# A compression of overlapping blocks in a two-layer attention trunk: each token stored once, and three weight chunks split earlier

## The chip, the cores and the metric

The kernel runs on one core of one Trainium2 chip. The metric is the time of one execution in microseconds (us), the median of several runs. Before the change it is 596.03 us (three runs, 595.75 to 596.15).

The core has five engines that work side by side, each through its own queue in order: TensorE (PE) multiplies matrices, with a separate unit for loading the stationary operand (PEld); VectorE (DVE), ScalarE (ACT) and GpSimd (POOL) work element by element; SyncE (SP) issues most of the DMA transfers.

## The reference

A trunk of two layers on 256 tokens of width 1024, in float32. Layer 0 is sparse latent attention with a squared-ReLU MLP. After it a shared key/value side is computed once from the normalized stream `hs`; layer 1 (attention over compressed, selected and window keys, again with an MLP) reads it. The change lies in that shared side:

```
kv = (hs @ w_kv).reshape(B, T, 6, N_KV_GROUPS, HEAD_DIM)
k_cmp, v_cmp, k_slc, v_slc, k_win, v_win = [kv[:, :, i] for i in range(6)]
kc = compress_blocks(k_cmp, n_cmp, pos_k, w1_k, w2_k)
vc = compress_blocks(v_cmp, n_cmp, pos_v, w1_v, w2_v)
...
def compress_blocks(raw, n_cmp, pos, w1, w2):
    idx = CMP_STRIDE * np.arange(n_cmp)[:, None] + np.arange(CMP_LEN)[None, :]
    blocks = raw[:, idx] + pos[None, None, :, None, :]
    flat = ...                       # (B, n_cmp, groups, CMP_LEN * HEAD_DIM)
    return jax.nn.gelu(flat @ w1) @ w2
```

There are 15 blocks of 32 tokens, each starting 16 tokens after the one before, so a token lies in two blocks (at place l and at place l - 16). Two groups make 30 blocks for the keys and 30 for the values. `w1` has 32 x 128 rows and 256 columns.

## The kernel before

Every float32 product is made of three matmuls: each operand is split into a rounded part (`h`, a cast on ScalarE) and a remainder (`l`, a subtraction on VectorE, `x - h`), and `h*h + h*l + l*h` is summed in PSUM (`mm3`). A weight chunk of 128 x 1024 is loaded by SyncE into one of five raw buffers (`rawp`), cast by ScalarE, and its remainder is taken by VectorE into one of eight buffers (`wp`). A raw buffer is free for the next load when the remainder has been written. The program order is made by a scheduler on the basis of its own costs; `behind(a, b)` lays down that `a` stands behind `b` on its engine.

The shared side runs as follows (function `trunk`):

- `kk`: keys of the selected and window branches, 96 matmuls with the four chunks `wk`; the scale `Rb` per token comes from the sum of squares of `x2`.
- The `xns` loop (line 850): eight products of `x2` by `Rb` on GpSimd into two alternating buffers, each split into `ah` (ScalarE) and `al` (VectorE), which the gates and the queries of layer 1 read later.
- `Ks` (lines 857 to 863): `kf` = `kk` times `Rb` on VectorE, cast on ScalarE, remainder on GpSimd.
- For kv = 0 (keys) and 1 (values), line 869: `kc`, 48 matmuls with the chunks `wc` into a bank of 512 columns (two groups of 256 tokens). `ff` (line 879) copies them out, times `Rb`, sorted by place in the block: for each of 32 places 30 columns of blocks, one of the position vector (line 881) and one of zeros. Four products of 16 x 15 elements do that, since each token stands at two places. `fr` holds the cast and the remainder of `ff`, 64 columns to a place; `fl` is a copy of the last place with 64 zero columns behind it, because a matmul takes 128 columns.
- `compress(kv, c, co)` (line 892): eight chunks of `cmp_w1`, of four places each. A place is one matmul: 128 columns of `fr` stationary, 512 columns (cast and remainder of the weights) moving, all summed in the bank `co`. Of the 128 result rows the first 64 are wanted. In the trace `c` are the split weights, `c1raw` their raw buffers. The remainders of kv 0's chunks 1 to 7 stand behind the remainder of `fr` of kv 0 (`frl[0]`).
- Behind it the V projection: four chunks `wv` of 12 matmuls each in the banks `v`, and between them kv 1's eight compression chunks. `compressed` copies 64 rows of `co` out (`cs`), and `hidden` sums the rows that belong together with the 0/1 matrix `sel` (matmuls `hp`), then the gelu; `kcT` is the compressed key.
- Then the gates (`gps`, 16 matmuls), the queries (`nq`, chunks `wq`) and the attention of layer 1.

`turn_gates` also uses `sel`, to sum two rows of each gate.

Of the kernel before, what the change touches and what calls it, by code (L numbers as in the profile page):

```python
# [50 lines left out]
def trunk(ctx: ExitStack, tc: tile.TileContext, I, out):  # L51
    nc = tc.nc
    const = ctx.enter_context(tc.tile_pool(name="const", bufs=1))
# [140 lines left out]
    def bcast(col2, name):  # L194

        ps = bank(name + "_ps")
        for i in range(2):
            mm(ps[:, i * P:(i + 1) * P], col2[:, i:i + 1].to_broadcast([P, P]), ident,
               i == 0, i == 1)
        b = kept([P, T], name)  # L200
        nc.vector.tensor_copy(b, ps[:, :T])
        return b
# [47 lines left out]
    for j in range(4):  # L250
# [8 lines left out]
        else:  # L259
# [4 lines left out]
            for a in range(2):  # L264
                g = vec[:, V_GA + 2 * j + a:V_GA + 2 * j + a + 1]
# [3 lines left out]
        for i in range(2):  # L269
            for a in range(2):  # L270
                k = 2 * j + a
# [23 lines left out]
    for j in range(2):  # L295
# [3 lines left out]
    pos = const.tile([P, 2, 32], F32, name="pos")  # L299
    pin(nc.sync.dma_start(pos, I["pos"]))  # L300
    pin(nc.sync.dma_start(biasT, bass.AP(tensor=u_ap.tensor, offset=u_ap.offset,
                                         ap=[[1, P], [384, H], [1, T]])))
    sel = const.tile([64, 32], F32, name="sel")
    pin(nc.sync.dma_start(sel, I["sel"]))


# [99 lines left out]
    for a in range(2):  # L406
        g = vec[:, V_GQ + a:V_GQ + a + 1]
# [361 lines left out]
    x1 = bigt([P, KT, T], F32, "x1")  # L769
# [9 lines left out]
    for fi in range(NF):  # L779
# [8 lines left out]
        if fi == 14:  # L788


            ps = bank("m1_ps")
# [9 lines left out]
        if 18 <= fi < 26:  # L801
            k = fi - 18
# [30 lines left out]
    for k in range(KT):  # L833
# [12 lines left out]
        if k == 6:  # L846
            Rb = bcast(r2, "Rb")

    xns = wk("cs", 1, [P, 2, T], "xns")
    for k in range(KT):  # L850
        xn = xns[:, k % 2]
        nc.gpsimd.tensor_tensor(xn, x2[:, k], Rb, op=OP.mult)
        hi, lo = split_gain(ah, al, x2, V_GA + 8, k, xn)
        behind(hi, kw_last[0])
        behind(lo, kw_last[1])
    Ks = bigt([P, 2, G, 2, T], F32R, "Ks")

    kf = x1[:, 4:].rearrange("p (g a) t -> p g a t", g=G)
    for g in range(G):
        nc.vector.tensor_tensor(kf[:, g], kk[g].rearrange("p (a t) -> p a t", a=2),  # L860
                                Rb[:, None, :].to_broadcast([P, 2, T]), op=OP.mult)
    nc.scalar.copy(Ks[:, 0], kf)
    nc.gpsimd.tensor_sub(Ks[:, 1], kf, f(Ks[:, 0]))


    w2 = wk("w2", 1, [P, 2, 2, P], "w2")
# [1 line left out]
    frs, frl = [], []  # L868
    for kv in range(2):
        ps = bank(f"kc{kv}")  # L870
        for g in range(G):
            projT(ps[:, g * T:(g + 1) * T], cw[2 * kv + g], sh, sl, g == 0)

        ff = x1[:, 4 * kv:4 * kv + 4].rearrange("p k t -> p (k t)").rearrange("p (l c) -> p l c", c=32)
        pv = ps.rearrange("p (g c b) -> p b g c", g=G, b=16)
        rv = Rb.rearrange("p (c b) -> p b c", b=16)
        for a in range(2):
            for g in range(G):
                nc.vector.tensor_tensor(ff[:, 16 * a:16 * a + 16, NCMP * g:NCMP * (g + 1)],
                                        pv[:, :, g, a:a + NCMP], rv[:, :, a:a + NCMP], op=OP.mult)  # L880
        nc.vector.tensor_copy(ff[:, :, 30:31], pos[:, kv, :, None])
        nc.vector.memset(ff[:, :, 31:32], 0.0)

        fr = bigt([P, 32, 2, 32], F32R, f"fr{kv}")
        nc.scalar.copy(fr[:, :, 0], ff)
        frl.append(nc.vector.tensor_sub(fr[:, :, 1], ff, f(fr[:, :, 0])))
        fl = wk("fl", 2, [P, 4, 32], f"fl{kv}", F32R)
        nc.gpsimd.memset(fl[:, 2:].bitcast(mybir.dt.int32), 0)
        nc.vector.tensor_copy(fl[:, :2], f(fr[:, 31]))
        frs.append((fr.rearrange("p l s c -> p (l s c)"), fl.rearrange("p s c -> p (s c)")))  # L890

    def compress(kv, c, co):
        fr, fl = frs[kv]
        raw = rawp.tile([P, 1024], F32, tag="raw", name=f"c1raw{kv}{c}")
        nc.sync.dma_start(raw, I["cmp_w1"][kv, c])
        w = wp.tile([P, 2, 1024], F32R, tag="w", name=f"c1{kv}{c}")
        w4 = w.rearrange("p a (b c) -> p (a b) c", c=512).rearrange("p l (s n) -> p l s n", s=2)
        r4 = raw.rearrange("p (l n) -> p l n", n=256)
        nc.scalar.copy(w4[:, :, 0], r4)
        lo = nc.vector.tensor_sub(w4[:, :, 1], r4, f(w4[:, :, 0]))  # L900
        if kv == 0 and c > 0:
            behind(lo, frl[0])
        for j in range(4):
            l = 4 * c + j
            mm(co, fr[:, 64 * l:64 * l + P] if l < 31 else fl, w4[:, j].rearrange("p s n -> p (s n)"),
               l == 0, l == 31)

    def compressed(kv, co):
        cs = wk("cs", 1, [64, 512], f"cs{kv}")
        nc.scalar.copy(cs, co[:64])  # L910
        return cs

    def hidden(kv, cs):
# [17 lines left out]
    co = [bank(f"co{kv}", acc=True) for kv in range(2)]  # L931
    for c in range(8):
        compress(0, c, co[0])
# [7 lines left out]
    for c in range(4):  # L941
        h, l = weights(I["kvV"][c], f"wv{c}")
        for i in range(2):
            for j in range(2):
                k = 2 * c + j
# [10 lines left out]
    ps = bank("kcT_ps")  # L956
# [11 lines left out]
    w4 = w[:, 0, :KT * 64].rearrange("p (k s c) -> p k s c", s=2, c=32)  # L968
# [7 lines left out]
    gT = wk("grep", 1, [64, T], "gT")  # L976
# [3 lines left out]
    def turn_gates():  # L980

        gtp = bank("gtp")
        for i in range(2):
            mm(gtp[:, i * 32:i * 32 + 24], gT[:, i * P:(i + 1) * P], sel[:, :24], i == 0, i == 1)
        gflat = gate.rearrange("p i h c -> p i (h c)")
        for i in range(2):
            nc.scalar.activation(gflat[:, i], gtp[:, i * 32:i * 32 + 24], AF.Exp, scale=-1.0)
        nc.vector.tensor_scalar(gflat, gflat, 1.0, None, op0=OP.add)
        nc.vector.reciprocal(gflat, gflat)
# [167 lines left out]
    ps = bank("vc_ps")  # L1157
# [4 lines left out]
    pv = ps[:, :T].rearrange("p (g d) -> p g d", g=G)  # L1162
# [45 lines left out]
    for fi in range(NF):  # L1208
# [14 lines left out]
        if 16 <= fi < 20:  # L1223
            i, c = divmod(fi - 16, 2)
            ps = bank(f"x3t{i}{c}")
# [19 lines left out]
    for i in range(2):  # L1245
        for c in range(2):
# [5 lines left out]
            if c == 0:  # L1252
                ins = nc.gpsimd.tensor_tensor(xg[:, i], x4[:, i, :512], gf[:, 0, :512], op=OP.mult)
# [27 lines left out]
def _const_arrays():  # L1281
    c = np.zeros((P, NC_), np.float32)
    c[:, C_ID:C_ID + P] = np.eye(P)
    p = np.arange(P)[:, None]
    s = np.arange(T)[None, :]
    c[:, C_CM:C_CM + T] = np.where(s > P + p, NEG, 0.0)
    n = np.arange(NCMP)[None, :]
    for i in range(2):
        ok = 16 * n + 31 <= i * P + p
        c[:, C_CA + 15 * i:C_CA + 15 * (i + 1)] = np.where(ok, 0.0, NEG)  # L1290
        c[:, C_C1 + 15 * i:C_C1 + 15 * (i + 1)] = ok
    for a in range(2):
        c[:, C_OWN + a] = 0.5 * (np.arange(P) % 32 // 16 == a)

    dist = np.arange(256)
    bucket = np.where(dist < 16, dist, 0)
    for b, lo in enumerate((16, 23, 32, 46, 64, 91, 128, 182)):
        bucket = np.where(dist >= lo, 16 + b, bucket)
    oh = np.zeros((32, 256), np.float32)
    oh[bucket, dist] = 1.0  # L1300
    sel = np.zeros((64, 32), np.float32)
    for j in range(30):
        sel[j, j] = sel[32 + j, j] = 1.0
    sel[30, :30] = sel[62, :30] = 1.0
    return c, oh, sel


# [72 lines left out]
```

## Time and profile before

| | |
|---|---|
| median of three runs | 596.03 us (595.75 to 596.15) |
| profiled execution | 595.66 us, of which 593.9 us are the span of the trace |
| TensorE busy | 577.7 us (97%) |
| VectorE, ScalarE, GpSimd busy | 366.2, 320.7, 155.9 us |
| granted TensorE clock | 0.998 of full speed |
| DMA | 103.96 MB, mean 175 GB/s |

A busy share says how long an engine had an instruction in it; a matmul whose operand comes late can count as busy. "Idle before" an instruction names what ended the wait. The chain that ended last follows the work back from the last instruction, at each step to what released it.

### The profile page before, as it was taken

The numbers are of one execution on the slowest core, as the hardware profiler recorded it, in microseconds if no ns is written. First come the engines' busy times: TensorE is split into PE (matmuls) and PEld (weight loads), VectorE is DVE, ScalarE is ACT, GpSimd is POOL, SyncE is SP. The second block draws the span as 40 slices with busy tenths as digits, with TensorE's granted clock in tenths as the row PEclk, the third lists the DMA queues.
The fourth block names the chain that finished last, engine by engine and source line by source line (L and its number), as shares of the span: only waits on it lengthen the run. The fifth ranks groups of instructions, "written<-read, shape, count | busy, mean of one in ns | idle before, by whom it ended". The sixth has DMA issues, their size and how long they took to land.

```text
span 593.9 us, 10855 instructions
## 1 busy us (share of the span) xinstructions
PE 577.7 (97%) x4170; PEld 542.6 (91%) x4170; DVE 366.2 (62%) x621; ACT 320.7 (54%) x580; POOL 155.9 (26%) x226
## 2 busy tenths in 40 slices
PE   8999999999999999999979999999999999999995
PEld 6788899999999999999958999999899998999994
DVE  4897399444475454447897877739845444444523
ACT  6656666454444444446576778627544445454423
POOL 0155466011011101014510067808410101011012
PEclk9999999999999999999999999999999999999999
DMA  8911448766556655544289843213866665566201
GB/s 306 338 51 57 162 159 256 240 179 187 174 160 197 201 175 187 178 142 159 73 302 315 318 174 108 78 66 129 278 205 185 195 183 173 181 178 197 84 1 71
DMA packets 30483, 103.96 MB, mean 175 GB/s; under 512 B 3640, under 2 KB 5472, under 8 KB 30304
## 3 DMA queue, kind: packets, MB, share of 16 engines
q1 hardware_dynamic: 30032, 102.45, 53.2%
q10 hardware_dynamic: 400, 0.83, 0.5%
q8 instruction: 32, 0.52, 0.3%
q14 instruction: 19, 0.16, 0.1%
HBM read 102.21 MB, written 1.06 MB: 174 GB/s over the span
## 4 chain that ended last, share of the span: by engine, by line
PE 84%; DVE 9%; issue 2%; DMA 2%; ACT 2%; POOL 1%; SPq 1%; POOLq 0%; ACTq 0%; DVEq 0%
PE y L94 30%; PE u L94 28%; PE nq L94 4%; PE yb L94 3%; PE ya L94 3%; PE kk L94 2%; PE npo L94 2%; PE v L94 1%; PE nl L94 1%; PE co L94 1%; DMA win_raw<-in_a_w_in 1%; PE kc L94 1%; PE ix L94 1%; DVE c L900 1%; DVE h0l L160 1%
## 5 line engine op out<-in xcount | busy, mean ns | idle before, releaser
L142 DVE TENSOR_TENSOR dn<-dn_raw,dn 128x1024 fp32r<-128x1024 f32 x64 | 80.7, 1260 | 99.1 <-ACT dn L141 99.1
L645 POOL TENSOR_TENSOR us<-ur 128x256 f32<-128x256 f32 x64 | 45.2, 708 | 282.2 <-ACT ur L642 282.2
L142 DVE TENSOR_TENSOR up<-up_raw,up 128x1024 fp32r<-128x1024 f32 x64 | 82.5, 1289 | 45.1 <-ACT up L141 45.1
L141 ACT CAST up<-up_raw 128x1024 fp32r<-128x1024 f32 x64 | 67.0, 1047 | 60.6 <-PE y L94 58.3
L94 PE MATMUL u<-h1h,up 128*128 128x256 f32 x512 | 97.0, 284 | 0.6 <-DVE up L142 0.6
L94 PE MATMUL y<-uu,dn 128*128 128x256 f32 x768 | 97.0, 283 | 0.2 <-DVE uu L647 0.2
L94 PE MATMUL u<-h0h,up 128*128 128x256 f32 x512 | 96.7, 283 | 0.0
L94 PEld LDWEIGHTS y<-uu,dn 128*128 128x128 f32 x768 | 94.2, 192 | 0.5 <-DVE uu L647 0.5
L94 PE MATMUL y<-dn,uu 128*128 128x512 f32 (+1 forms) x396 | 92.5, 384 | 0.0
L94 PEld LDWEIGHTS u<-h1h,up 128*128 128x128 f32 x512 | 81.5, 191 | 1.6 <-DVE up L142 0.8
L94 PEld LDWEIGHTS y<-dn,uu 128*128 128x128 f32 x396 | 71.1, 189 | 13.0
L642 ACT ACTIVATE ur<-u 128x256 f32<-128x256 f32 x64 | 24.5, 383 | 106.8 <-PE u L94 106.8
L94 PEld LDWEIGHTS u<-h0h,up 128*128 128x128 f32 x512 | 81.7, 192 | 0.0
L94 PE MATMUL u<-h1l,up 128*128 128x256 f32 x256 | 72.5, 283 | 0.0
L94 PE MATMUL u<-h0l,up 128*128 128x256 f32 x256 | 72.2, 283 | 0.0
L141 ACT CAST dn<-dn_raw 128x1024 fp32r<-128x1024 f32 x64 | 66.8, 1043 | 7.3 <-PE y L94 2.9
L94 PEld LDWEIGHTS u<-h1l,up 128*128 128x128 f32 x256 | 49.0, 191 | 0.9
L94 PEld LDWEIGHTS u<-h0l,up 128*128 128x128 f32 x256 | 49.1, 192 | 0.0
L647 DVE TENSOR_TENSOR uu<-us,uu 128x256 fp32r<-128x256 f32 x64 | 29.1, 454 | 8.1 <-POOL us L645 8.1
L646 ACT ACTIVATE uu<-ur 128x256 fp32r<-128x256 f32 x64 | 26.7, 417 | 0.1
L94 PE MATMUL ya<-oT,wo 128*128 128x256 f32 x192 | 25.2, 288 | 0.3 <-DVE oT L591 0.3
L94 PE MATMUL yb<-nTh,wn 128*128 128x256 f32 x128 | 24.7, 284 | 0.1
(304 smaller groups left out, 966.8 us busy)
## 6 DMA issues: line engine op xcount, KB each, us to landing
up_raw<-in_w_up SPq DMA_DIRECT2D x64, 512.0 KB, 3.7
dn_raw<-in_w_down SPq DMA_DIRECT2D x64, 512.0 KB, 3.7
c1raw<-in_cmp_w SPq DMA_DIRECT2D x16, 512.0 KB, 4.7
wo_raw<-in_a_w_o SPq DMA_DIRECT2D x8, 512.0 KB, 4.3
wq_raw<-in_b_w_q SPq DMA_DIRECT2D x8, 512.0 KB, 6.0
wn_raw<-in_b_w_o SPq DMA_DIRECT2D x8, 512.0 KB, 4.9
wk_raw<-in_kvT SPq DMA_DIRECT2D x4, 512.0 KB, 3.6
wc_raw<-in_kvT SPq DMA_DIRECT2D x4, 512.0 KB, 3.6
```

What stands on the lines that cost most here:

```text
L94: return nc.tensor.matmul(ps, a, b, start=start, stop=stop, skip_group_check=True)
L141: ins = [hi(w[:, 0, :C], raw[:, :C]) if hi else nc.scalar.copy(w[:, 0, :C], raw[:, :C]), (lo or nc.vector).tensor_sub(w[:, 1, :C], raw[:, ...
L142: (lo or nc.vector).tensor_sub(w[:, 1, :C], raw[:, :C], f(w[:, 0, :C]))]
L160: nc.vector.scalar_tensor_tensor(dst_l[:, k], x, g, f(dst_h[:, k]), op0=OP.mult, op1=OP.subtract))
L642: nc.scalar.activation(r, ps[:, :T], AF.Relu)
L645: nc.gpsimd.tensor_tensor(s, r, r, op=OP.mult)
L646: nc.scalar.activation(u[:, 0], r, AF.Square)
L647: nc.vector.tensor_sub(u[:, 1], s, f(u[:, 0]))
L900: lo = nc.vector.tensor_sub(w4[:, :, 1], r4, f(w4[:, :, 0]))
```

## The change

The tokens are sorted by their place modulo 16 and stored once: `ff` is one product of 16 x 2 x 16 elements, with two position columns (places l and l + 16) behind each 32, thus 34 columns for each of 16 places. `fr` has 17 rows of 2 x 34 columns, the last of zeros. Place l of the blocks reads 128 columns from `68 * (l % 16) + l // 16`: for l from 16 on the window is shifted by one column, which is the next block. The wanted rows become 68, and `sel` is rebuilt for them (with columns of its own for the gates). `fl` goes. The remainder of `Ks` is taken on VectorE. The remainders of kv 0's chunks 1 and 2 need no longer stand behind `frl[0]`; `al` from the third on stands behind it, and from the fifth on behind `frl[1]`; kv 1's `ff` stands behind `frl[0]`.

```diff
-    sel = const.tile([64, 32], F32, name="sel")
+    sel = const.tile([68, 56], F32, name="sel")
...
+    als = []
     for k in range(KT):
         xn = xns[:, k % 2]
         nc.gpsimd.tensor_tensor(xn, x2[:, k], Rb, op=OP.mult)
         hi, lo = split_gain(ah, al, x2, V_GA + 8, k, xn)
         behind(hi, kw_last[0])
         behind(lo, kw_last[1])
+        als.append(lo)
...
     nc.scalar.copy(Ks[:, 0], kf)
-    nc.gpsimd.tensor_sub(Ks[:, 1], kf, f(Ks[:, 0]))
+    nc.vector.tensor_sub(Ks[:, 1], kf, f(Ks[:, 0]))
...
-        ff = x1[:, 4 * kv:4 * kv + 4].rearrange("p k t -> p (k t)").rearrange("p (l c) -> p l c", c=32)
-        pv = ps.rearrange("p (g c b) -> p b g c", g=G, b=16)
-        rv = Rb.rearrange("p (c b) -> p b c", b=16)
-        for a in range(2):
-            for g in range(G):
-                nc.vector.tensor_tensor(ff[:, 16 * a:16 * a + 16, NCMP * g:NCMP * (g + 1)],
-                                        pv[:, :, g, a:a + NCMP], rv[:, :, a:a + NCMP], op=OP.mult)
-        nc.vector.tensor_copy(ff[:, :, 30:31], pos[:, kv, :, None])
-        nc.vector.memset(ff[:, :, 31:32], 0.0)
-
-        fr = bigt([P, 32, 2, 32], F32R, f"fr{kv}")
-        nc.scalar.copy(fr[:, :, 0], ff)
-        frl.append(nc.vector.tensor_sub(fr[:, :, 1], ff, f(fr[:, :, 0])))
-        fl = wk("fl", 2, [P, 4, 32], f"fl{kv}", F32R)
-        nc.gpsimd.memset(fl[:, 2:].bitcast(mybir.dt.int32), 0)
-        nc.vector.tensor_copy(fl[:, :2], f(fr[:, 31]))
+        ff = x1f[:, 544 * kv:544 * (kv + 1)].rearrange("p (b c) -> p b c", c=34)
+        ins = nc.vector.tensor_tensor(ff[:, :, :32].rearrange("p b (g c) -> p b g c", g=G),
+                                      ps.rearrange("p (g c b) -> p b g c", g=G, b=16),
+                                      Rb.rearrange("p (c b) -> p b c", b=16)[:, :, None, :].to_broadcast([P, 16, G, 16]),
+                                      op=OP.mult)
+        if kv:
+            behind(ins, frl[0])
+        nc.vector.tensor_copy(ff[:, :, 32:34], pos[:, kv].rearrange("p (a b) -> p b a", a=2))
+
+        fr = bigt([P, 17, 2, 34], F32R, f"fr{kv}")
+        nc.gpsimd.memset(fr[:, 16].bitcast(mybir.dt.int32), 0)
+        nc.scalar.copy(fr[:, :16, 0], ff)
+        frl.append(nc.vector.tensor_sub(fr[:, :16, 1], ff, f(fr[:, :16, 0])))
+        for lo in als[2 + 2 * kv:]:
+            behind(lo, frl[kv])
...
-        if kv == 0 and c > 0:
+        if kv == 0 and c > 2:
             behind(lo, frl[0])
         for j in range(4):
             l = 4 * c + j
-            mm(co, fr[:, 64 * l:64 * l + P] if l < 31 else fl, w4[:, j].rearrange("p s n -> p (s n)"),
+            o = 68 * (l % 16) + l // 16
+            mm(co, fr[:, o:o + P], w4[:, j].rearrange("p s n -> p (s n)"),
                l == 0, l == 31)
```

VectorE's queue before, from chunk 0's remainder to chunk 3's (`c_3494` is chunk 0 of kv 0, `c_3503` chunk 1, `c_3512` chunk 2, `c_3521` chunk 3; `x_850` holds `kf` and `ff`):

```order
L900 TENSOR_TENSOR c_3494<-c1raw_3492,c_3494 128x4x256
L201 COPY Rb<-Rb_ps 128x256
L860 TENSOR_TENSOR x_850<-kk_3186,Rb 128x512
L860 TENSOR_TENSOR x_850<-kk_3187,Rb 128x512
L160 SCALAR_TENSOR_TENSOR al<-xns,vec,ah 128x256 x2
L879 TENSOR_TENSOR x_850<-kc_3368,Rb 128x16x15 x4
L160 SCALAR_TENSOR_TENSOR al<-xns,vec,ah 128x256 x2
L886 TENSOR_TENSOR fr_3423<-x_850,fr_3423 128x32x32
L881 COPY x_850<-pos 128x32
L900 TENSOR_TENSOR c_3503<-c1raw_3501,c_3503 128x4x256
L900 TENSOR_TENSOR c_3512<-c1raw_3510,c_3512 128x4x256
L900 TENSOR_TENSOR c_3521<-c1raw_3519,c_3521 128x4x256
```

The same piece of VectorE's queue now (chunks 0 to 3 are `c_3482`, `c_3491`, `c_3500`, `c_3509`):

```order
L903 TENSOR_TENSOR c_3482<-c1raw_3480,c_3482 128x4x256
L201 COPY Rb<-Rb_ps 128x256
L903 TENSOR_TENSOR c_3491<-c1raw_3489,c_3491 128x4x256
L863 TENSOR_TENSOR x_850<-kk_3186,Rb 128x512
L863 TENSOR_TENSOR x_850<-kk_3187,Rb 128x512
L903 TENSOR_TENSOR c_3500<-c1raw_3498,c_3500 128x4x256
L160 SCALAR_TENSOR_TENSOR al<-xns,vec,ah 128x256 x2
L866 TENSOR_TENSOR Ks<-x_850,Ks 128x1024
L879 TENSOR_TENSOR x_850<-kc_3368,Rb 128x16x32
L885 COPY x_850<-pos 128x16x2
L890 TENSOR_TENSOR fr_3419<-x_850,fr_3419 128x16x34
L160 SCALAR_TENSOR_TENSOR al<-xns,vec,ah 128x256 x2
```

The remainders of chunks 1 and 2 moved from behind `fr` to between `Rb` and the first `al`, the `Ks` remainder came onto this queue, and four `ff` products became one.

TensorE's queue where the first `wv` chunk is used, before (`v_3567` and `v_3568` are the two V banks; `fr` of kv 0 is stationary in `co_3490`):

```order
L94 MATMUL co_3490<-c_3539,fr_3423 128x512 x4
L94 MATMUL v_3567<-wv_3571,sh 128x512
L94 MATMUL v_3568<-wv_3571,sh 128x512
L94 MATMUL co_3490<-c_3548,fr_3423 128x512 x4
L94 MATMUL co_3490<-c_3557,fr_3423 128x512 x3
L94 MATMUL co_3490<-c_3557,fl_3426 128x512
```

and now:

```order
L94 MATMUL co_3478<-c_3527,fr_3419 128x512 x4
L94 MATMUL co_3478<-c_3536,fr_3419 128x512 x4
L94 MATMUL v_3555<-wv_3559,sh 128x512
L94 MATMUL v_3556<-wv_3559,sh 128x512
L94 MATMUL co_3478<-c_3545,fr_3419 128x512 x4
```

Seven chunks of kv 0 stand ahead of the first two V matmuls in place of six, and the matmul with `fl` reads `fr` like the others. The number of matmuls is the same. SyncE issues the loads in the same order as before.

## Rows read from the trace of the kernel before

**Rows 1.** Table by stretch: time, then each engine's busy time (instructions), clock, DMA share.

```profile
core 0: us, PE busy (x) PEld busy (x) DVE busy (x) ACT busy (x) POOL busy (x), PEclk, DMA share, GB/s
293.10:325.48 32.38, 29.01 (x127) 21.72 (x126) 29.33 (x37) 20.18 (x27) 1.86 (x3) 1.00 0.84 287
325.48:402.00 76.52, 76.39 (x625) 74.87 (x624) 54.00 (x149) 50.73 (x129) 35.99 (x57) 1.00 0.45 150
```

**Rows 2.** Timeline of TensorE: start, us, instructions, and the idle time before them.

```profile
293.10 6.67 PE L94 MATMUL co<-c,fr 128*128 128x512 f32 x24
...
302.31 0.73 PE L94 MATMUL v<-wv,sh 128*128 128x512 f32 x2 [2.55 <-ACT wv L141]
...
308.19 0.73 PE L94 MATMUL v<-wv,sh 128*128 128x512 f32 x2 [0.82 <-ACT wv L141]
...
325.48 0.28 PE L94 MATMUL gps<-ah,wg 128*128 128x256 f32 x1
```

**Rows 3.** Chain that ended last, 286 to 326 us: start, us, what.

```profile
302.47 4.52 DMA wv_raw<-in_kvV
...
308.92 1.00 PE hp L94 x8
...
315.16 0.45 PE v L94 x2
...
316.52 2.27 PE v L94 x10
318.78 0.91 PE co L94 x4
...
321.05 0.36 PE kcT_ps L94 x4
```

**Rows 4.** Timeline of SyncE's DMA issues.

```profile
282.59 0.33 SPq L895 DMA_DIRECT2D c1raw<-in_cmp_w  x1
294.03 1.47 SPq L895 DMA_DIRECT2D c1raw<-in_cmp_w  x2
296.32 0.33 SPq L139 DMA_DIRECT2D wv_raw<-in_kvV  x1
```

**Rows 5.** Timeline of ScalarE: the casts of chunks 0 to 3, of chunk 6, of `wv`.

```profile
280.26 3.90 ACT L899 CAST c<-c1raw 128x1024 fp32r<-128x1024 f32 x4 [4.24 <-PE kk L94]
...
297.64 1.05 ACT L899 CAST c<-c1raw 128x1024 fp32r<-128x1024 f32 x1 [4.31 <-DMA c1raw<-in_cmp_w]
...
301.22 1.04 ACT L141 CAST wv<-wv_raw 128x1024 fp32r<-128x1024 f32 x1 [0.52 <-DMA wv_raw<-in_kvV]
```

**Rows 6.** Timeline of VectorE, from chunk 0's remainder to chunk 5's.

```profile
281.34 1.23 DVE L900 TENSOR_TENSOR c<-c1raw,c 128x1024 fp32r<-128x1024 f32 x1 [3.02 <-ACT c L899]
...
282.94 1.29 DVE L860 TENSOR_TENSOR x<-kk,Rb 128x512 f32<-128x512 f32 x2
...
287.54 2.08 DVE L879 TENSOR_TENSOR x<-kc,Rb 128x240 f32<-128x240 f32 x4 [0.90 <-PE kc L94]
289.53 0.99 DVE L160 SCALAR_TENSOR_TENSOR al<-xns,vec,ah 128x256 fp32r<-128x256 f32 x2
290.73 1.47 DVE L886 TENSOR_TENSOR fr<-x,fr 128x1024 fp32r<-128x1024 f32 x1 [0.21 <-ACT fr L885]
292.12 0.73 DVE L881 COPY x<-pos 128x32 f32<-128x32 f32 x1
...
293.89 4.62 DVE L900 TENSOR_TENSOR c<-c1raw,c 128x1024 fp32r<-128x1024 f32 x4
```

**Rows 7.** Timeline of GpSimd in the same stretch.

```profile
282.98 0.74 POOL L852 TENSOR_TENSOR xns<-x,Rb 128x256 f32<-128x256 f32 x1 [3.88 <-DVE Rb L201]
...
287.41 2.43 POOL L863 TENSOR_TENSOR Ks<-x,Ks 128x1024 fp32r<-128x1024 f32 x1
290.20 0.91 POOL L852 TENSOR_TENSOR xns<-x,Rb 128x256 f32<-128x256 f32 x1 [0.36 <-DVE al L160]
291.08 1.71 POOL L852 TENSOR_TENSOR xns<-x,Rb 128x256 f32<-128x256 f32 x1
```

**Rows 8.** Groups of TensorE's weight loads, 293.1 to 325.48 us: busy us, mean ns.

```profile
L94 PEld LDWEIGHTS co<-c,fr 128*128 128x128 f32 x62 | 11.1, 188 | 3.8 <-DVE c L900 1.8
```

More of the change, by code (lines that the diff above doesn't have):

```diff
@@ L855, in trunk @@
         behind(lo, kw_last[1])
+        als.append(lo)
     Ks = bigt([P, 2, G, 2, T], F32R, "Ks")
+    x1f = x1.rearrange("p k t -> p (k t)")
     kf = x1[:, 4:].rearrange("p (g a) t -> p g a t", g=G)
@@ L872, in trunk @@
             projT(ps[:, g * T:(g + 1) * T], cw[2 * kv + g], sh, sl, g == 0)
-        ff = x1[:, 4 * kv:4 * kv + 4].rearrange("p k t -> p (k t)").rearrange("p (l c) -> p l c", c=32)
-        pv = ps.rearrange("p (g c b) -> p b g c", g=G, b=16)
-        rv = Rb.rearrange("p (c b) -> p b c", b=16)
-        for a in range(2):
-            for g in range(G):
-                nc.vector.tensor_tensor(ff[:, 16 * a:16 * a + 16, NCMP * g:NCMP * (g + 1)],
-                                        pv[:, :, g, a:a + NCMP], rv[:, :, a:a + NCMP], op=OP.mult)
-        nc.vector.tensor_copy(ff[:, :, 30:31], pos[:, kv, :, None])
-        nc.vector.memset(ff[:, :, 31:32], 0.0)
-        fr = bigt([P, 32, 2, 32], F32R, f"fr{kv}")
-        nc.scalar.copy(fr[:, :, 0], ff)
-        frl.append(nc.vector.tensor_sub(fr[:, :, 1], ff, f(fr[:, :, 0])))
-        fl = wk("fl", 2, [P, 4, 32], f"fl{kv}", F32R)
-        nc.gpsimd.memset(fl[:, 2:].bitcast(mybir.dt.int32), 0)
-        nc.vector.tensor_copy(fl[:, :2], f(fr[:, 31]))
-        frs.append((fr.rearrange("p l s c -> p (l s c)"), fl.rearrange("p s c -> p (s c)")))
+        ff = x1f[:, 544 * kv:544 * (kv + 1)].rearrange("p (b c) -> p b c", c=34)
[12 more added lines that the diff above has]
+            behind(lo, frl[kv])
+        frs.append(fr.rearrange("p l s c -> p (l s c)"))
     def compress(kv, c, co):
-        fr, fl = frs[kv]
+        fr = frs[kv]
         raw = rawp.tile([P, 1024], F32, tag="raw", name=f"c1raw{kv}{c}")
@@ L904, in compress @@
             l = 4 * c + j
-            mm(co, fr[:, 64 * l:64 * l + P] if l < 31 else fl, w4[:, j].rearrange("p s n -> p (s n)"),
+            o = 68 * (l % 16) + l // 16
+            mm(co, fr[:, o:o + P], w4[:, j].rearrange("p s n -> p (s n)"),
                l == 0, l == 31)
     def compressed(kv, co):
-        cs = wk("cs", 1, [64, 512], f"cs{kv}")
-        nc.scalar.copy(cs, co[:64])
+        cs = wk("cs", 1, [68, 512], f"cs{kv}")
+        nc.scalar.copy(cs, co[:68])
         return cs
@@ L983, in turn_gates @@
         for i in range(2):
-            mm(gtp[:, i * 32:i * 32 + 24], gT[:, i * P:(i + 1) * P], sel[:, :24], i == 0, i == 1)
+            mm(gtp[:, i * 32:i * 32 + 24], gT[:, i * P:(i + 1) * P], sel[:64, 32:56], i == 0, i == 1)
         gflat = gate.rearrange("p i h c -> p i (h c)")
@@ L1300, in _const_arrays @@
     oh[bucket, dist] = 1.0
-    sel = np.zeros((64, 32), np.float32)
+    sel = np.zeros((68, 56), np.float32)
     for j in range(30):
-        sel[j, j] = sel[32 + j, j] = 1.0
-    sel[30, :30] = sel[62, :30] = 1.0
+        r = j // 15 * 16 + j % 15
+        sel[r, j] = sel[34 + r, j] = 1.0
+    sel[32, :30] = sel[66, :30] = 1.0
+    for j in range(24):
+        sel[j, 32 + j] = sel[32 + j, 32 + j] = 1.0
     return c, oh, sel
```

## The prediction

> **What bounds the kernel now.** I read the table of busy time by stretch first, then TensorE's timeline in the one stretch that stands out, then the chain of waits through it, then the timelines of the queues that the chain names.
>
> TensorE is at 29.01 us of 32.38 us in the stretch from 293.10 to 325.48 us, while the DMA engines are at 0.84 of their time and VectorE at 29.33 us; in the 76.5 us behind it TensorE lacks only 0.13 us [rows 1]. So whatever brings the start of the stage behind (325.48 us, the first `gps` matmul) forward should reach the end almost one for one.
>
> In the stretch TensorE stands still for 2.55 and for 0.82 us, both times until ScalarE has cast a `wv` chunk [rows 2]. The busy time hides a third loss: 24 `co` matmuls take 6.67 us, though four of them need 0.91 us when nothing holds them, thus 5.4 us for 24. The work in the stretch, from the chain's pieces [rows 3]: 16 compression chunks of 0.91 are 14.6, four V chunks of 0.45 + 2.27 are 10.9, `hp` 1.00 and `kcT` 0.36, together 26.8. So 32.4 - 26.8 = 5.6 us are lost here. That is the ceiling of any gain in this stretch.
>
> Why it waits: the chain goes through the DMA of a `wv` chunk, 4.52 us [rows 3]. The loads share five raw buffers, so a load is issued when the remainder of the chunk five loads before it is written. SyncE issues the load of compression chunk 5 at 282.59 us and the next only at 294.03 [rows 4]: 11.4 us of silence, because remainders 1 and 2 sit on VectorE behind the whole chain kf, `ff`, `fr` (282.94 to 292.85) [rows 6]. ScalarE then waits 4.31 us for chunk 6 and casts the first `wv` at 301.22 [rows 5].
>
> **The change part by part.** I follow VectorE, the engine whose order is changed, in starts (its instructions overlap a little: a 1.23 us remainder takes 1.15 from start to start, 4 in 4.62 [rows 6]).
>
> *Three remainders first.* ScalarE has cast chunks 0 to 3 by 284.16 [rows 5], so nothing holds them. Remainder 0 from 281.34, `Rb` to 282.94 as now, remainder 1 to 284.1, kf 1.3 to 285.4, remainder 2 to 286.5. Loads 6 and 7 then go out at 284.1 and 286.5 in place of 294.03 and 295.2.
>
> *Ks remainder on VectorE.* GpSimd's 2.43 us [rows 7] go; nothing waited for them. On VectorE it is 1024 elements from SBUF, as a chunk's remainder: 1.15. With two `al` (0.45 each, from 0.99 for two) VectorE is at 288.5.
>
> *ff and fr.* Four multiplications of 240 elements, 2.08 us, become one of 512 with the same 16-element steps in PSUM. Bounds: the contiguous kf product, 0.65 for 512, and 512 at the old rate, 512/240 x 0.52 = 1.1. I take 1.05, as the step is the same. `fr` has 544 columns in place of 1024: the cast lies between 0.5 and 1.05, the remainder between the 0.45 of 256 elements and 1.15; by size 0.65 and 0.7. So `fr` of kv 0 stands at 288.5 + 1.05 + 0.65 + 0.7 = 290.9, in place of 292.2. TensorE is busy with `kc` until 293.10 anyway: this gains nothing by itself, and 2.2 us of cover are left. The dropped `fl` and fill instructions (0.2 us each at most) count for nothing. The padded columns are zeroed on idle GpSimd. The 32 positions go in one copy as before; now it cost 0.73 (below), and waiting for the `fr` cast covers it.
>
> *The chain behind.* Two `al` to 291.8; remainders 3 to 6 at 293.0, 294.1, 295.3, 296.5. TensorE eats chunks 0 to 6 from 293.1 without a hole and is through at 293.1 + 7 x 0.91 = 299.5. The first `wv` load goes out when remainder 3 is done, 293.0 in place of 296.32; a load took 3.6 us (chunk 6) to 4.9 (`wv`) [rows 4, 5], so it lands by 296.7 to 297.9 and is cast by 299.0: in time. VectorE goes on: `ff` of kv 1 297.5, remainder 7 298.7, `wv` 299.9, `fr` 300.6, two `al` 301.5, then v-side chunks and `wv` at 1.15 each with two `al` between: 302.7, 303.8, 305.0, 306.6, 308.2, 309.4. TensorE: V chunk 0 complete at 303.1 (0.45, chunk 7, 2.27), kv 1 chunks 0 and 1 at 305.4, V chunk 1 at 307.7, then the third `wv` cast. Its load hangs on remainder 302.7, so it is cast about 302.7 + 3.6 to 4.9 + 1.05 = 307.4 to 308.7, up to 1 us late. From there 0.45 + 2 x 0.91 + 1.00 + 2.27 + 0.91 + 0.45 + 0.91 + 2.27 + 2 x 0.91 = 11.9 us bring the last chunk to 319.6 to 320.6, say 320.1, and `kcT` follows (0.36): 320.5 against 325.48. That is 5.0 us with no cost for sharing.
>
> Do the loads keep up? Chunks 6, 7 and the first `wv` landed within 301.22 - 297.64 us, 1.79 each [rows 5]. Eleven more loads from 296.7 end at 316.4; with cast, remainder and matmuls 1.05 + 1.15 + 0.91 that is 319.5, just before TensorE is there. The loads are no bound, but without margin.
>
> *The shared ports.* GpSimd's second `xns` product of the pair took 1.71 us where one alone took 0.74, beside a VectorE remainder that took 1.47, and the position copy ends only when that product ends (291.08 + 1.71) [rows 6, 7]. So an instruction of VectorE that reads two tensors in SBUF and one of GpSimd that reads SBUF take turns. Now remainders 1 and 2, Ks and 3 to 7 all stand beside an `xns`, where Ks used to be on the same queue as `xns` and could not collide with it. Six `xns` of about 0.6 each would cost VectorE 3.6 us by the time of kv 1; TensorE's cover there is 1 to 2 us. At the stage's end that is about 2.0 us, and 0 where no turn collides. I take half, 1.0: gain 5.0 - 1.0 = 4.0.
>
> The Trainium skill (SBUF — State Buffer, Who interferes with whom) states that a VectorE instruction with two SBUF inputs contends with a GpSimd instruction that reads SBUF, and that the loser is blocked to the end of the other; this trace agrees (1.71 against 0.74 us). It speaks against putting the Ks remainder on VectorE here: by it the gain would be the lower one, 3.0.
>
> *Behind 325.48.* The order of `nq`, `nl` and `yb` on TensorE shifts by a few instructions, none added. The `wq` loads hang on the same remainders and move with them. I cost it at 0, give or take 0.5. The `sel` load grows from 64x32 to 68x56 in a queue at the kernel's start; 0.
>
> Sum: 595.66 in the profiled execution, which is its span of 593.9 and 1.8 outside it, less 4.0: 591.7. The median before is 596.03, 0.4 above the profiled execution, so 592.0 for the runs.
>
> **Rivals.**
> 1. *The ports decide every time.* The turns are taken at each of six `xns`, VectorE's chain is 2 us later at V chunk 2, TensorE waits for remainders instead of loads: gain 3.0, 593.0. For it: the 1.71 and 1.47 rows. Against: an `xns` starts only when an `al` two before it is done, so some fall beside products from PSUM, which read SBUF once.
> 2. *Hidden and given back.* The stationary operand `fr` is now read from offsets that are no multiple of 64, half of them odd. No row shows such a load. A `co` weight load takes 188 ns [rows 8] under 227 ns of matmul, so 39 ns are free; were odd ones to take twice that, 32 of 64 would cost 149 ns each, 4.8 us, the gain would be gone and the time 596 to 597. Against: the operand stays contiguous along the 128 columns. The same time results if loads, at 0.84 of the DMA engines, cannot go faster.
> 3. *Slower: the strided product.* The position copy writes 32 elements in 0.73 us, 23 ns each [rows 6]. If that is the price of scattered writing and not of the ports, `ff` of 512 elements costs 11.7 us in place of 2.08. Both products lie in VectorE's chain before kv 1's first chunk, where the cover is 2 us at most. So it decides once two products cost 2.0 + 4.0 us more than I count, from 1.05 + 3.0 = 4.0 us each; at 11.7 the chain is 2 x 10.65 = 21 us longer, 19 after the cover, and the time 592 + 19 = 611. Against: four 240-element products with the same steps ran at 2.2 ns per element.
>
> **How the numbers follow.** Forecast 0.62 (own range 590.6 to 593.0); no sharing at all and a better fit, down to 590.4, is in it. Rival 1 0.18, rival 2 0.12, rival 3 0.08. A measurement of this kernel tells about 0.2%, 1.2 us, from no change. The forecast and rival 1 are faster by more: 0.80; rival 2 is the same, 0.12; rival 3 slower, 0.08. The range runs from the ceiling, 596.03 - 5.6 = 590.4, to 594.6, which takes in rival 1 and a part of what lies towards rival 2.
>
> **What would show it.** Right: the load of chunk 6 issued near 284 and the first `wv` near 293; first `wv` cast by 299; 24 `co` matmuls in 5.4 us; `gps` or `nq` at 321 to 323; one `ff` near 1.05 us. Rival 1: TensorE waits on VectorE remainders, and `xns` above 1 us at each remainder. Rival 2: `co` weight loads above 227 ns. Rival 3: an `ff` above 3 us. My forecast is wrong if the first `wv` is still cast after 301, or if the stage behind 325.48 gets longer by more than 1 us.

## The result, and the profile after

The changed kernel takes 593.28 us (median of seven runs, 592.47 to 594.39); the kernel before took 596.15 us on the same chip (seven runs, 595.75 to 599.48). The ratio is 0.9940, with a 95% interval of 0.9925 to 0.9955: 0.6% faster. On 596.03 us the ratio is 592.5 us, the interval 591.6 to 593.3. So the forecast (592.0) and Rival 1 (593.0) both lie inside it, and only the traces can tell which of them holds. On a second chip the ratio was 0.9928 (0.9910 to 0.9947).

The size of the gain depends on what is compared: 3.6 us by the ratio, 2.9 by the two medians above, 2.4 by the two profiled executions. In 38 of the 43 executions of the kernel before that stand beside the experiments below, the mean granted TensorE clock was 0.991 to 0.995, in its profiled one 0.998, and in all 13 executions of the changed kernel 0.996 to 0.998; so a ratio can hold some time of the clock that the stretch read below does not show.

The profiled execution took 593.29 us, of which 591.5 us are the span.

By stretch (time, then each engine's busy time; to be held against [rows 1]):

```profile
293.10:322.50 29.40, 28.02 (x126) 22.16 (x125) 27.59 (x30) 20.50 (x27) 6.65 (x5) 1.00 0.86 285
322.50:402.00 79.50, 79.37 (x649) 77.72 (x648) 54.75 (x154) 52.14 (x131) 38.57 (x60) 1.00 0.44 149
```

TensorE, timeline of the stretch (start, us, instructions, idle before; against [rows 2]):

```profile
293.49 6.67 PE L94 MATMUL co<-c,fr 128*128 128x512 f32 x28
...
305.31 0.73 PE L94 MATMUL v<-wv,sh 128*128 128x512 f32 x2 [1.26 <-ACT wv L141]
...
310.29 0.74 PE L94 MATMUL v<-wv,sh 128*128 128x512 f32 x2
...
322.39 0.28 PE L94 MATMUL nq<-ah,wq 128*128 128x256 f32 x1
322.51 0.28 PE L94 MATMUL nq<-al,wq 128*128 128x256 f32 x1
...
322.99 0.36 PE L94 MATMUL gps<-ah,wg 128*128 128x256 f32 x1
```

28 `co` matmuls now take the 6.67 us that 24 took, and one wait for a cast of `wv` is left, 1.26 us, where there were two of 2.55 and 0.82. From the first `co` to the first `gps` it is 322.99 - 293.49 = 29.50 us; two `nq` matmuls (0.24) now stand ahead of `gps`, so 29.26 against 32.38: 3.1 us gained. The stretch began 0.4 us later than before (293.49 against 293.10), in a part that the change does not touch; over all kernels with the early remainders below it began between 292.96 and 293.71. From `gps` to the end of the span it is 268.5 us, with the two `nq` 268.7, before 593.9 - 325.48 = 268.4. Thus 3.1 - 0.4 - 0.3 = 2.4, the difference of the two profiled executions.

SyncE's loads, and ScalarE's casts of the first three `wv` chunks (against [rows 4, 5]):

```profile
284.45 2.71 SPq L898 DMA_DIRECT2D c1raw<-in_cmp_w  x2
294.28 0.33 SPq L139 DMA_DIRECT2D wv_raw<-in_kvV  x1
295.95 1.48 SPq L898 DMA_DIRECT2D c1raw<-in_cmp_w  x2
298.18 0.33 SPq L139 DMA_DIRECT2D wv_raw<-in_kvV  x1
```

```profile
297.71 1.05 ACT L141 CAST wv<-wv_raw 128x1024 fp32r<-128x1024 f32 x1 [2.37 <-DMA wv_raw<-in_kvV]
304.21 1.05 ACT L141 CAST wv<-wv_raw 128x1024 fp32r<-128x1024 f32 x1 [1.31 <-DMA wv_raw<-in_kvV]
309.19 1.05 ACT L141 CAST wv<-wv_raw 128x1024 fp32r<-128x1024 f32 x1 [0.33 <-DMA wv_raw<-in_kvV]
```

Chunks 6 and 7 are loaded at 284.45 and 286.83 us (before 294.03 and 295.2), the first `wv` is cast at 297.71 (before 301.22). The second `wv` load is the late one: it is issued at 298.18 and cast 6.0 us later.

VectorE and GpSimd (against [rows 6, 7]):

```profile
287.88 1.39 DVE L866 TENSOR_TENSOR Ks<-x,Ks 128x1024 fp32r<-128x1024 f32 x1 [0.29 <-ACT Ks L865]
289.20 1.05 DVE L879 TENSOR_TENSOR x<-kc,Rb 128x512 f32<-128x512 f32 x1
290.16 0.19 DVE L885 COPY x<-pos 128x32 f32<-128x32 f32 x1
291.00 0.73 DVE L890 TENSOR_TENSOR fr<-x,fr 128x544 fp32r<-128x544 f32 x1 [0.65 <-ACT fr L889]
291.65 0.88 DVE L160 SCALAR_TENSOR_TENSOR al<-xns,vec,ah 128x256 fp32r<-128x256 f32 x2
292.44 5.71 DVE L903 TENSOR_TENSOR c<-c1raw,c 128x1024 fp32r<-128x1024 f32 x4
298.08 1.05 DVE L879 TENSOR_TENSOR x<-kc,Rb 128x512 f32<-128x512 f32 x1
```

```profile
292.27 2.53 POOL L853 TENSOR_TENSOR xns<-x,Rb 128x256 f32<-128x256 f32 x2 [2.38 <-DVE al L160]
302.57 4.79 POOL L853 TENSOR_TENSOR xns<-x,Rb 128x256 f32<-128x256 f32 x2 [7.77 <-DVE al L160]
```

Remainders 3 to 6 take 5.71 us where four took 4.62. A pair of `xns` takes 2.4 to 4.8 us; the mean of the eight is 1555 ns, before 919. The remainder of chunk 6 ends at 298.15, and the second `wv` load goes out at 298.18.

The weight loads of `co` in the same stretch (count, busy us, mean ns; against [rows 8]), half of them now from odd offsets:

```profile
L94 PEld LDWEIGHTS co<-c,fr 128*128 128x128 f32 x64 | 11.9, 188 | 2.8
```

### The profile page after: what moved, and what is told of

It is laid out like the page before. It is cut to its first block, busy times and chain, and to the rows that moved or that the text cites. A ratio compares the mean times of both kernels' runs of the same rounds, so it can differ in the third digit from the quotient of the medians.

```text
span 591.5 us, 10852 instructions
## 1 busy us (share of the span) xinstructions
PE 577.2 (98%) x4170; PEld 542.9 (92%) x4170; DVE 364.2 (62%) x612; ACT 320.4 (54%) x580; POOL 159.1 (27%) x225
## 4 chain that ended last, share of the span: by engine, by line
PE 84%; DVE 9%; issue 2%; DMA 2%; ACT 1%; POOL 1%; SPq 1%; POOLq 0%; ACTq 0%; DVEq 0%
PE y L94 30%; PE u L94 28%; PE nq L94 4%; PE yb L94 3%; PE ya L94 3%; PE kk L94 2%; PE npo L94 2%; PE kc L94 1%; PE nl L94 1%; DVE c L903 1%; DMA win_raw<-in_a_w_in 1%; PE v L94 1%; PE co L94 1%; PE ix L94 1%; DMA wv_raw<-in_kvV 1%
## 5 line engine op out<-in xcount | busy, mean ns | idle before, releaser
L94 PE MATMUL nq<-ah,wq 128*128 128x256 f32 x128 | 24.9, 286 | 0.0
```

## The experiments

The theory drawn from this profile: the early remainders give the gain, by earlier loads, and the shared ports take about 2 us of it back, through the load that hangs on the remainder of chunk 6. Rivals: the `Ks` remainder on VectorE costs it; the loads alone set the stage (the DMA engines are at 0.86 of their time), and the ports cost nothing. Four kernels ran on one chip (before: 597.25 us, 20 runs), four on another (before: 596.93 us, 12 runs), two more on a third (before: 597.74 us, 11 runs).

**The Ks remainder back on GpSimd.**

```diff
-    nc.vector.tensor_sub(Ks[:, 1], kf, f(Ks[:, 0]))
+    nc.gpsimd.tensor_sub(Ks[:, 1], kf, f(Ks[:, 0]))
```

> The changed kernel with the Ks remainder back on GpSimd; the rest as changed. The scheduler then puts one al behind remainders 3 to 6. Ports theory (VectorE and GpSimd take turns at SBUF, and this delays the remainders that free raw buffers): the Ks remainder of 1.39 us leaves VectorE's queue, but GpSimd's 2.4 us of Ks now stand beside the fr remainder and an al, so the first wv load moves by less than 1 us either way and the time stays within 0.8 us of the changed kernel (ratio to before 0.993 to 0.996). If the turns do not matter and only the length of VectorE's queue does: the wv load goes out 1.4 us earlier (about 292.9) and the time falls by 1 us (ratio 0.992).

593.98 us (593.72 to 594.43), ratio 0.9946 (0.9928 to 0.9965). The same time as the change. VectorE gets to `ff` 1.05 us earlier, and the `fr` remainder behind it then waits for ScalarE's cast and lies beside `Ks` on GpSimd:

```profile
288.15 1.07 DVE L879 TENSOR_TENSOR x<-kc,Rb 128x512 f32<-128x512 f32 x1 [0.33 <-PE kc L94]
290.22 1.15 DVE L890 TENSOR_TENSOR fr<-x,fr 128x544 fp32r<-128x544 f32 x1 [1.00 <-ACT fr L889]
```

That remainder takes 1.15 us in place of 0.73. What leaves VectorE comes back as a wait and as a collision, and in the time this part of the change is worth nothing that can be measured. The stretch of this one execution, which begins at 293.71, does not say the same:

```profile
323.82 0.36 PE L94 MATMUL gps<-ah,wg 128*128 128x256 f32 x1
```

Without the 17 `nq` that stand ahead of `gps` here (2.0 us) it is 28.1 us, 1.2 less than in the change, while the part behind it is 0.5 longer. One `al` came to stand behind remainders 3 to 6 with this edit, and the second `wv` load goes out at 297.46. Whether `Ks` or that `al` shortened the stretch, and why the time is no shorter, this run does not show.

**The early remainders alone.** The kernel before with

```diff
-        if kv == 0 and c > 0:
+        if kv == 0 and c > 2:
```

> The kernel before with nothing changed but that the remainders of chunks 1 and 2 need not stand behind the fr remainder. If the gain comes from the loads that go out earlier: chunk 6 is issued near 284 instead of 294, the first wv near 294.5 instead of 296.3, and most of the gain is there, 1.5 to 2.5 us of the 3.6 (ratio 0.996 to 0.9975); the rest, about 1 to 1.5 us, is the longer ff and fr on VectorE (2 x 1.0 and 2 x 0.5 us). If the gain comes from the smaller layout, this gives less than 0.7 us (ratio above 0.999).

594.57 us (594.28 to 595.99), ratio 0.9961 (0.9945 to 0.9977): 2.3 us of the 3.6 by the ratios. The first `wv` load goes out at 294.07 and is cast at 297.42, as in the change. What TensorE waits for is now VectorE itself (total us, times, longest):

```profile
PE co L94 <- DVE fr L886: 1.4, 1, 1.4
PE co L94 <- DVE c L900: 1.3, 1, 1.3
```

These are kv 1's `fr` and chunk 7 of kv 0, behind four `ff` products of 2.04 us and remainders of 1024 columns. In the stretch, which begins at 293.25, the gain is smaller than by the ratio:

```profile
324.20 0.36 PE L94 MATMUL gps<-ah,wg 128*128 128x256 f32 x1
```

With one `nq` (0.1) taken off it is 30.8 us, 1.6 below the kernel before, half of the change's 3.1.

**The layout alone.** The kernel before with the new `ff`, `fr` and `sel`, and everything else as it was.

```diff
+    sel = const.tile([68, 56], F32, name="sel")
...
+        fr = bigt([P, 17, 2, 34], F32R, f"fr{kv}")
...
         if kv == 0 and c > 0:
             behind(lo, frl[0])
```

> The kernel before with the tokens stored once and the shifted columns alone: remainders of chunks 1 to 7 stand behind the fr remainder as before, Ks remainder on GpSimd as before, no new order for al or ff. If the loads' early issue makes the gain: chunk 6 is still issued only when remainder 1 is done, near 292.5, and the time falls by 0.7 to 1.5 us (ratio 0.9975 to 0.999), by the 1 us of VectorE that ff saves before it. If the layout makes the gain: 2.5 us or more (ratio under 0.996).

596.29 us (595.21 to 597.71), ratio 0.9987 (0.9973 to 1.0000): 0.8 us by the ratio, and by its interval between nothing and 1.6. The silence of SyncE stays, and with it the wait for `wv`:

```profile
284.33 12.31 SPq L894 DMA_DIRECT2D c1raw<-in_cmp_w  x3
297.46 0.33 SPq L139 DMA_DIRECT2D wv_raw<-in_kvV  x1
```

```profile
304.16 1.22 PE L94 MATMUL v<-wv,sh 128*128 128x512 f32 x2 [3.25 <-ACT wv L141]
```

The granted clock fell behind this wait. In this execution (597.52 us, the median is 596.29) the table by stretch shows it at 0.50, the 1.2 GHz level, and TensorE's timeline shows eight `co` matmuls that take 2.02 us in the change:

```profile
304.16:307.20 3.04, 3.04 (x7) 2.46 (x8) 3.04 (x5) 3.04 (x5) 0.00 (x0) 0.50 0.87 305
```

```profile
305.18 2.94 PE L94 MATMUL co<-c,fr 128*128 128x512 f32 x8
```

As an estimate, 3.04 us at half the clock cost 1.5 us. The mean granted clock of this kernel's executions was 0.991 to 0.996, much as that of the kernel before beside it. So the wait for `wv` seems to cost more than its own length in most executions of both; that the clock falls at the same place in the kernel before is not shown, since its only profiled execution stayed at 1.00 there.

The change stands 1.3 us (0.9961 to 0.9940) below the early remainders alone, though the two intervals, from two chips, overlap; and the two waits for VectorE are gone. The layout may thus be worth more once the remainders are early. But the change also moves `Ks`, six `al` and kv 1's `ff`, so how much of this is the layout's is not shown.

**GpSimd without reads.** The `xns` products become fills, so that GpSimd reads no SBUF beside the remainders. The kernel leaves out the product: the gates and queries of layer 1 come from a constant. `Ks` is held behind the second `al`, where it stood in the change.

```diff
-        nc.gpsimd.tensor_tensor(xn, x2[:, k], Rb, op=OP.mult)
+        after_sync(nc.gpsimd.memset(xn, 0.5), rb_ins[-1])
...
-    nc.vector.tensor_sub(Ks[:, 1], kf, f(Ks[:, 0]))
+    behind(nc.vector.tensor_sub(Ks[:, 1], kf, f(Ks[:, 0])), als[1])
```

> The changed kernel in which the eight xns products on GpSimd are fills of a constant, issued after Rb as the products are: GpSimd writes SBUF there and reads nothing, so gates and queries of layer 1 come from a constant. Ports theory: remainders 3 to 6 take 4.6 us in place of 5.7, Ks 1.2 in place of 1.4, the load of the second wv goes out 1.5 us or more earlier than its 298.2, TensorE's wait of 1.26 us at the second wv nearly goes, and the time falls by a further 1.0 to 1.8 us (ratio 0.991 to 0.9925). Rival theory (what is left is the loads' landing, the second wv took 6.0 us, since several loads share the DMA engines): the remainders may get shorter, but the wait stays above 0.8 us and the time falls by less than 0.5 us.

591.43 us (590.51 to 592.86), ratio 0.9907 (0.9886 to 0.9929), 2.0 us below the change by the ratios, from two chips, and a little more than expected. VectorE, SyncE and TensorE in that run:

```profile
291.31 4.62 DVE L905 TENSOR_TENSOR c<-c1raw,c 128x1024 fp32r<-128x1024 f32 x4
```

```profile
295.96 0.33 SPq L139 DMA_DIRECT2D wv_raw<-in_kvV  x1
```

```profile
292.96 6.67 PE L94 MATMUL co<-c,fr 128*128 128x512 f32 x28
...
320.25 0.28 PE L94 MATMUL gps<-ah,wg 128*128 128x256 f32 x1
```

The four remainders are back at 4.62 us, the second `wv` load is 2.2 us earlier, and TensorE waits for no `wv`. From the first `co` to the first `gps` it is 27.3 us, of which one `nq` is 0.2: 27.1 against 29.26 with the products, so 2.2 us. The fills are also shorter than products, so `al` comes earlier too. This run alone does not say that it is the reads.

**Extra reads, extra fills.** Two kernels whose instruction order on the other four engines is that of the change. GpSimd, idle from 294.8 to 302.6 us, gets six instructions whose result nobody reads, between the sixth and the seventh `xns` product (`xin`).

```diff
+    prev = xin[0]
+    for k in range(6):
+        e = nc.gpsimd.tensor_tensor(x1f[:, 1600:1856], x2[:, k], Rb, op=OP.mult)
+        behind(e, prev)
+        prev = e
+    behind(xin[1], prev)
```

In the second kernel the product is `nc.gpsimd.memset(x1f[:, 1088:1856], 0.5)`.

> The changed kernel with six extra products on GpSimd between the sixth and the seventh xns product, each reading two tensors of 128x256 in SBUF and writing scratch that nobody reads. The order on every other engine is that of the changed kernel, and GpSimd is idle there (294.8 to 302.6 us). The changed kernel stands at 0.994 of before. Theory (the shared ports): the two products beside remainders 3 to 6 made these take 5.71 us in place of 4.62, some 0.5 each; five or six more fall beside remainders 4 to 6 and cost VectorE 1.5 to 3 us, so the remainder of chunk 6 ends at 299.6 to 301, the second wv load (298.18) goes out as much later, and the time is 1 to 2.5 us more than the changed kernel's: ratio to before 0.9955 to 0.999. Rival (the loads alone set the stage, the ports cost nothing): remainders 4 to 6 unchanged, ratio 0.992 to 0.995.

> The same place, but six fills of 128x768 (a constant, written to scratch) in place of the six products: GpSimd is about as busy but reads nothing. Theory (ports are taken by reads): remainders 3 to 6 as in the changed kernel, 5.6 to 5.8 us, ratio to before 0.992 to 0.995. Rival (any work of GpSimd beside VectorE costs, or its queue delays xns): as the run with extra reads, 0.9955 to 0.999.

With reads 595.22 us (594.89 to 595.52), ratio 0.9973 (0.9962 to 0.9984); with fills 593.28 us (592.81 to 593.35), ratio 0.9938 (0.9925 to 0.9951). With reads, GpSimd, VectorE and TensorE's waits:

```profile
294.29 9.25 POOL L872 TENSOR_TENSOR x<-x,Rb 128x256 f32<-128x256 f32 x6
```

```profile
291.96 6.82 DVE L912 TENSOR_TENSOR c<-c1raw,c 128x1024 fp32r<-128x1024 f32 x4
...
301.20 1.75 DVE L142 TENSOR_TENSOR wv<-wv_raw,wv 128x1024 fp32r<-128x1024 f32 x1
```

```profile
PE co L94 <- DVE c L912: 1.9, 3, 0.8
```

With fills:

```profile
294.84 4.73 POOL L872 MEMSET x<- 128x768 f32 x6
```

```profile
292.54 5.71 DVE L912 TENSOR_TENSOR c<-c1raw,c 128x1024 fp32r<-128x1024 f32 x4
```

Six products, each of 1.5 us where one alone took 0.74, cost 1.9 us against six fills at the same place. The remainders stand at 6.82 us with the reads, and with the fills at 5.71, the change's own figure. So it is GpSimd's reads that cost, and that the loads alone set the stage is refuted. By the Trainium skill (SBUF — State Buffer, Who interferes with whom) a VectorE instruction with two SBUF inputs contends with GpSimd's reads, not with a GpSimd instruction that only writes; these two traces agree on both halves.

**Late al.** A version that follows from this: the last six `al`, and with them the `xns` that they release, go behind the remainder of the second `wv` chunk. Kv 0's rows of `co` go to a free part of `x1`, since `cs` shares its buffer with `xns`.

```diff
-        for lo in als[2 + 2 * kv:]:
-            behind(lo, frl[kv])
...
-        cs = wk("cs", 1, [68, 512], f"cs{kv}")
+        cs = wk("cs", 1, [68, 512], f"cs{kv}") if kv else x1f[:68, 1088:1600]
...
+        if c == 1:
+            for lo in als[2:]:
+                behind(lo, w_last[1])
```

> The changed kernel, but the last six al stand behind the remainder of the second wv chunk (not behind fr), and kv 0's 68 rows of co are copied into a free part of x1 so that the xns buffer isn't needed for them. Theory (loads hang on the remainders, and those on the al ahead of them and the xns products beside them): two al (0.9 us) and two colliding xns (about 1.1) go from ahead of remainder 6, so the second wv load goes out at 296 to 297 in place of 298.18, its chunk is cast by 302 to 303 in place of 305.3, TensorE's wait for it (1.3 us) goes, and the third comes 2 us earlier too: 1 to 2 us less than the changed kernel, ratio to before 0.9905 to 0.9925. Rival (the DMA engines are at their limit, so earlier issue only makes the loads land as late): the wait stays at 1 us or more, ratio 0.993 to 0.995. A loss is possible where the late al hold up the gates at the stage's end: ratio above 0.995, with TensorE waiting at gps for al.

591.31 us (591.18 to 592.05), ratio 0.9909 (0.9896 to 0.9922). VectorE, SyncE, ScalarE, TensorE:

```profile
291.36 4.62 DVE L901 TENSOR_TENSOR c<-c1raw,c 128x1024 fp32r<-128x1024 f32 x4
```

```profile
296.02 0.33 SPq L139 DMA_DIRECT2D wv_raw<-in_kvV  x1
```

```profile
301.21 1.05 ACT L141 CAST wv<-wv_raw 128x1024 fp32r<-128x1024 f32 x1 [0.28 <-DMA wv_raw<-in_kvV]
```

```profile
293.21 6.67 PE L94 MATMUL co<-c,fr 128*128 128x512 f32 x28
...
320.62 0.28 PE L94 MATMUL gps<-ah,wg 128*128 128x256 f32 x1
```

All products are still made, some of them still slow (a pair takes 5.26 us from 309.28), but none stands beside remainders 3 to 6. The second `wv` is cast 3.0 us earlier than in the change, and the trace shows no wait of TensorE from 290 to 325 us. The stretch takes 27.41 us, 27.2 without two `nq`, as without reads.

**Late Ks as well.** The `Ks` remainder goes behind the remainder of chunk 6.

```diff
+        if kv == 0 and c == 6:
+            behind(ks_lo, lo)
```

> As the kernel with late al, and the Ks remainder stands behind the remainder of chunk 6 as well. Theory: ff, fr and remainders 3 to 6 start up to 1.3 us earlier (kc is complete at about 288, where ff now starts at 289.20), so the first wv load goes out at 292 to 293 and the second at 295 to 296: 0 to 1 us below the kernel with late al, ratio to before 0.989 to 0.992, and remainders 3 to 6 at the 4.6 us that they took before. Rival (the loads are the bound by now): the same time as with late al alone, within 0.3 us.

591.81 us (591.38 to 594.04), ratio 0.9923 (0.9908 to 0.9937): no gain over late `al` alone; by the medians it is 0.5 us more, and the intervals overlap. The second `wv` load goes out 1.0 us earlier, at 295.03, and is cast at 300.88, only 0.3 us earlier than with late `al`: the load itself took longer, which speaks for the rival. It is not shown that the loads are the only bound: in the profiled execution (594.04 us) TensorE also waits 1.08 us before `hp`, for a copy on ScalarE.

**The change and late al on one chip.**

The two kernels are those above, unchanged.

> The changed kernel itself once more, to stand on one chip beside the kernel with late al. Expected: ratio to before 0.9925 to 0.9955, as at first. If the ratio came out at 0.992 or less, the gain of the late al would be a difference between chips and not of the kernels.

> The changed kernel with the last six al behind the remainder of the second wv chunk, on the same chip as the changed kernel. Theory (two al, two colliding xns ahead of remainder 6 cost TensorE 1.3 us at the second wv chunk and the rest before the gates): 1.5 to 2.3 us less than the changed kernel, ratio to before 0.990 to 0.992. Rival (nothing but a difference of chips): within 0.7 us of the changed kernel.

The change: 593.65 us (592.63 to 594.13, six runs), ratio 0.9928 (0.9910 to 0.9947). Late `al`: 591.78 us (591.43 to 592.79, five runs), ratio 0.9903 (0.9884 to 0.9921). By the ratios 1.5 us, by the medians 1.9: it beats both kernels. The two intervals overlap a little, but only one run of the change (592.63) lies below a run of late `al` (592.79). In this trace of the change TensorE waits for a cast of `wv` twice, 0.6 us at the second chunk and 1.2 at the third; with late `al` not at all.

## Why the prediction was right, and where its size was off

The sign, the place and the mechanism were right; the gain was forecast as 4.0 us and came out at 3.1 in the stretch, 2.4 in the profiled executions and 3.6 by the ratio. That 592.5 by the ratio lies so near to 592.0 is in part luck: the shared ports cost more than the text took, and the ratio holds 1.2 us more gain than the two profiled executions do, for which the text had no term.

- *The ceiling.* 26.8 us of work in the stretch: the two kernels without collisions come to 27.1 and 27.2, so it stands.
- *Three remainders first.* Loads 6 and 7 were forecast at 284.1 and 286.5, the first `wv` load at 293.0 and its cast by 299.0. Measured 284.45, 286.83, 294.28 and 298.76. The early remainders alone bring 2.3 us by the ratio and 1.6 in the stretch, where the other parts bring as much again.
- *The `Ks` remainder, `ff`, `fr`.* Forecast 1.15, 1.05 and 0.7 us; measured 1.39, 1.05 and 0.73. `Ks` is 0.17 longer than without GpSimd's reads (1.22). That the layout gains nothing on the kv 0 side held, as `kc` covers `fr`. But kv 1's `ff` and `fr` have no such cover. In the text they are terms of VectorE's chain; their own worth was never worked out. The rest of the change is worth 1.3 us by the ratios and 1.6 in the stretch once the remainders are early, and the share of `ff` and `fr` in it is not shown.
- *The chain behind.* The text put the end without sharing at 320.5, or 27.4 us from the first `co`. The kernel without GpSimd's reads measures 27.1.
- *The shared ports: the term that was mis-sized.* The bounds were 0 and 2.0 us, and the text took half. Measured 2.2 us in the stretch (29.26 against 27.1), the upper bound and a little more; the shorter fills of that kernel are in this figure too. So the mechanism of Rival 1 decided: it said 3.0 us of gain, the stretch shows 3.1. The reason given against it, that an `xns` starts only when an earlier `al` is done and so may fall beside a product from PSUM, did not help: from the second pair on every `xns` was released by an `al`, and right behind two `al` VectorE had a remainder or `Ks` to do.
- *The sign named for Rival 1* was half right. `xns` is above 1 us, but TensorE waits for no remainder in the change: the late remainder of chunk 6 delays a load, and the wait appears as one for ScalarE's cast. Only with still more reads did the waits for remainders appear (1.9 us).
- *Loads.* "No bound, but without margin" held up to a point: late `al` gains from earlier issue, late `Ks` no more. A load was taken as 3.6 to 4.9 us from issue to cast; the second `wv` took 6.0, so its wait (1.26 us) is not the late issue alone, and it came one chunk before the one where the text looked for up to 1 us.
- *Rival 2* falls: `co` weight loads take 188 ns at all offsets, and the time did change. *Rival 3* falls: `ff` takes 1.05 us, and kv 0's position copy, which seemed to cost 23 ns an element, takes 0.19 us in place of 0.73.
- *Behind the stage* the forecast said 0, give or take 0.5; measured 0.3 us more.

## What to carry to other kernels

When transfers hang on buffers that an element-wise engine sets free, look at what stands ahead of the freeing instruction in that engine's queue, and let it pass whatever is due later: here two remainders came ahead of the chain to `fr`, and then six `al` went behind, each time for 1.5 to 2.3 us. Moving work also moves what it releases, so check which products on GpSimd it sets off, and beside which two-input instructions of VectorE they then run. Where a price for such a collision lies between nothing and every time, and the other engine's instruction is released by the one just ahead, take it as paid every time, as it was here.

## What the runs showed of the hardware

- Six fills on GpSimd (768 columns, 0.74 us each) left VectorE's remainders beside them at the change's own 5.71 us, while products of two tensors took 1.5 us each in place of 0.74 and stretched a remainder from 1.22 to 1.75.
- Kv 0's position copy of 32 elements took 0.73 us before, where it ended with GpSimd's product, and 0.19 in the change, where the pair of `xns` had ended 0.3 us ahead of it: the short instruction had waited for the long one.
- `ff` with a step of 16 elements in PSUM took 1.05 us for 512 columns, the contiguous `kf` product 0.68.
- TensorE's clock: behind the 3.25 us wait in the kernel with the layout alone the granted clock was 0.50, the 1.2 GHz level, for at least 3.0 us. In the profiled execution of the kernel with late `al` and late `Ks` TensorE stood still for 1.08 us before `hp`, and the clock was 0.50 soon after. The 2.55 us wait in the kernel before and the 1.26 us wait in the change left it at 1.00. What made the difference is open. TensorE's timeline and the table by stretch of the execution with late `Ks`:

```profile
305.11 1.08 PE L94 MATMUL hp<-sel,x 68*128 68x30 f32 x8 [1.08 <-ACT x L914]
```

```profile
306.70:308.50 1.80, 1.80 (x6) 1.37 (x5) 1.80 (x3) 1.80 (x6) 0.00 (x0) 0.50 0.54 132
```
